# Merge weights spread by one load for two heads, and the output weights loaded in halves: a one-core hybrid decoder step

## The chip, the cores and the metric

The kernel runs on one core of a Trainium2 chip. The metric is the device time of one launch in microseconds (us). The time before is the median of three runs, 3149.05 us (3148.02 to 3153.83). The profile belongs to one further execution, which took 3154.4 us.

## The reference

One layer computes three branches from a normalized input: attention with three dilated patterns per head (A), a convolution (B) and attention to 256 memory tokens (C). Each branch is gated, projected to 1024 columns and merged with a gate; the sum goes through `w_out`, a norm and the residual. Cut to what the change touches:

```python
# branch A: 12 heads of 64; per head three patterns (window, dilation) = (128,1), (512,4), (2048,16)
for (w, d) in PATTERNS:
    o, lse = _dilated_band(qa, ka, va, bias(d), d, w // d)     # o (B,S,H,Dh), lse (B,S,H)
    outs.append(o); lses.append(lse)
wgt = softmax(stack(lses), axis=0)                             # three merge weights per position and head
oa  = einsum('gbshd,gbsh->bshd', stack(outs), wgt)             # branch A's output
...
mix = (gates[..., 0, :] * ((oa * silu(za)) @ w_pa)
     + gates[..., 1, :] * ((ob * silu(zb)) @ w_pb)
     + gates[..., 2, :] * ((oc * silu(zc)) @ w_pc))
y = x + rmsnorm(mix @ w_out, g_post)                           # 2048 prompt rows and 32 sample rows, 1024 wide
```

## The kernel before, in words

Everything is float32. A product is made of three matmuls on a high and a low part of each operand (`gemm`, L166 to L168). The program has three phases. The first (to about 870 us) normalizes the input, makes q, k and v and the convolution's input. The second runs the memory attention, the sample attention and then branch A (about 1600 to 2560 us), while `sweep` fills TensorE's queue with the gate projections (tiles `gg`, weights `whi` and `wlo`, which GpSimd splits at L55 and L56). The third, `phase_c` (2520 us to the end), goes over the positions in four parts of 512 or 544. In each part the branches follow one another in the order C, B, A: the activations `araw` are loaded (L1136) and gated (L1139), split in two (`split_ad`, L1197 on ScalarE and L1198 on VectorE), and eight column blocks are multiplied by the projection weights `craw` (PSUM tile `pg`) and added to `mix` (L1150 to L1155). Then `mix` times `w_out` gives `y` (L1178 to L1180).

Branch A works on six pairs of heads (`att_pair`). A pair's two heads sit in partitions 0 to 63 and 64 to 127 of three tiles `O`, one per pattern. When both heads are done, the softmax statistics go through DRAM and come back as `stc`, and the merge weights `ew` are stored to the DRAM tensor `d_cf`, three rows of 2 x 2048 numbers (L441). They have to be spread: the 64 partitions of a head all need the same row. For each half of the positions (1024) and each pattern (3), a tile `cb` of 128 x 1024 is filled from `d_cf` by two loads, one per head, each of which reads one row of 1024 numbers 64 times (L448). `cb` has two buffers. VectorE multiplies `O` by `cb` for patterns 0 and 1, GpSimd for pattern 2 (L451), and VectorE adds the three (L452, L453) before the result is stored to `d_act` (L454). So a pair takes six `cb` tiles.

A scheduler fixes the order of instructions on each engine before the run; each engine then works through its own list in that order, and an instruction whose data isn't there holds up all behind it. Loads and stores are issued in the same manner: nearly all by SyncE (SP), some by ScalarE (`wraw` and the gates' stores). The next pair's attention starts while the last pair's merge is under way, so its instructions (score matmuls `s` L616 and L617, VectorE's `T` at L625, transposes `pt`, products `o`, splits `pl` at L576, additions to `O` at L644) stand among the merge's on the same engines. The score tiles `s` have two PSUM buffers.

`w_out` (4 MB) is loaded in the first part, after branch A's column blocks in the program text: eight loads of 512 KB into the two buffers of `xr`, each split by ScalarE (L1166) and VectorE (L1167). `xr` also serves the residual input later (L1183).

Of the kernel before, what the change touches and what calls it, by code (L numbers as in the profile page):

```python
# [7 lines left out]
F32 = mybir.dt.float32  # L8
R32 = mybir.dt.float32r
AF = mybir.ActivationFunctionType  # L10
# [5 lines left out]
D = 1024  # L16
S = 2048
# [20 lines left out]
class K:  # L38
# [379 lines left out]
    def att_pair(self, hp):  # L418
        nc, ap, ps, ao = self.nc, self.ap, self.aps, self.ao
        Oraw = [ao.tile([128, S], F32, name="O", bufs=4) for p in range(3)][::-1]  # L420
        bias = self.bias_tiles(hp, ap, ps)
        for a in range(2):
            self.att_head(hp, a, Oraw, {p: t[:, a] for p, t in bias.items()})

        st = ao.tile([32, 6, 128], F32, name="stc")
        for a in range(2):
            nc.sync.dma_start(st[16 * a:16 * a + 16], self.d_st[2 * hp + a].rearrange("g (r i) -> r g i", i=128))
        mn = ao.tile([32, 128], F32, name="mn")
        nc.vector.tensor_tensor(mn, st[:, 0, :], st[:, 1, :], op=ALU.min)
        nc.vector.tensor_tensor(mn, mn, st[:, 2, :], op=ALU.min)  # L430
        e = ao.tile([32, 3, 128], F32, name="ew")
        nc.vector.tensor_tensor(e, st[:, 0:3, :], mn[:, None, :].to_broadcast([32, 3, 128]), op=ALU.subtract)
        nc.scalar.activation(e, e, AF.Exp, scale=-1.0)
        el = st[:, 3:6, :]
        nc.vector.tensor_mul(el, e, el)
        w = ao.tile([32, 128], F32, name="wsum")
        nc.vector.tensor_add(w, el[:, 0, :], el[:, 1, :])
        nc.vector.tensor_add(w, w, el[:, 2, :])
        nc.vector.reciprocal(w, w)
        nc.vector.tensor_tensor(e, e, w[:, None, :].to_broadcast([32, 3, 128]), op=ALU.mult)  # L440
        nc.sync.dma_start(self.d_cf[hp].rearrange("g (q i) -> q g i", i=128), e)  # L441
        for half in range(2):
            cs = slice(half * 1024, half * 1024 + 1024)
            for g in range(3):
                cb = ao.tile([128, 1024], F32, name="cb", bufs=2)
                for a in range(2):
                    src = self.d_cf[hp][g:g + 1, a * S + half * 1024:a * S + half * 1024 + 1024]
                    nc.sync.dma_start(cb[64 * a:64 * a + 64, :],  # L448
                                      bass.AP(tensor=src.tensor, offset=src.offset, ap=[[0, 64], [1, 1024]]))
                eng = nc.gpsimd if g == 2 else nc.vector  # L450
                eng.tensor_mul(Oraw[g][:, cs], Oraw[g][:, cs], cb)  # L451
            nc.vector.tensor_add(Oraw[0][:, cs], Oraw[0][:, cs], Oraw[1][:, cs])  # L452
            nc.vector.tensor_add(Oraw[0][:, cs], Oraw[0][:, cs], Oraw[2][:, cs])  # L453
            nc.sync.dma_start(self.d_act[hp][:, cs], Oraw[0][:, cs])  # L454
# [648 lines left out]
    def phase_c(self):  # L1103
        tc, nc, I, O = self.tc, self.nc, self.I, self.O
        PARTS = [(0, 512, [512]), (512, 512, [512]), (1024, 512, [512]), (1536, 544, [272, 272])]
        with tc.tile_pool(name="cm", side="right", bufs=1, reuse_waits="tile") as mp, \
# [9 lines left out]
            wo = []  # L1116
            xp = I["x_prompt"].rearrange("o (i r) d -> (o r) i d", r=16)
            yp = O["y_p"].rearrange("o (i r) d -> (o r) i d", r=16)
            for s, n, chs in PARTS:
# [11 lines left out]
                for bi, (br, k0, kb, wn) in enumerate(((2, 12, 4, "w_proj_c"), (1, 6, 6, "w_proj_b"), (0, 0, 6, "w_proj_a"))):  # L1131
                    acts = []
                    gn = load_g(br, 0)
                    for k in range(kb):
                        raw = cp.tile([128, 544], F32, name="araw", bufs=2)
# [6 lines left out]
                    for cb in range(8):  # L1142
                        w = self.load_w(wp, I[wn][0, :, 128 * cb:128 * cb + 128], kb, "c", bufs=2, act=True)
                        gs = gn
                        o = 0
# [12 lines left out]
                            gn = load_g(br, cb + 1)  # L1158
                        if bi == 2:
                            mhl.append(self.split_ad(ap, mix[cb], n))  # L1160
                if not wo:
                    for k in range(8):
                        raw = yp_.tile([128, D], F32, name="xr", bufs=2)
                        nc.sync.dma_start(raw, I["w_out"][0, 128 * k:128 * k + 128, :])
                        h, l = ((op if k < 6 else yp_).tile([128, D], R32, name=f"wo{c}{k}") for c in "hl")
                        nc.scalar.activation(h, raw, AF.Copy)  # L1166
                        nc.vector.tensor_sub(l, raw, h.bitcast(F32))  # L1167
                        wo.append((h, l))
                for t0 in range(0, n, 128):
                    m = min(128, n - t0)  # L1170
                    tt = (s + t0) // 128
                    y = psy.tile([128, 2, 512], F32, name="y")
                    ts_ = slice(t0, t0 + m)
                    for c in range(2):
                        cs = slice(512 * c, 512 * c + 512)
                        for k in range(8):
                            (ah, al), (bh, bl) = mhl[k], wo[k]
                            nc.tensor.matmul(y[:m, c, :], ah[:, ts_], bh[:, cs], start=k == 0, stop=False)  # L1178
                            nc.tensor.matmul(y[:m, c, :], ah[:, ts_], bl[:, cs], start=False, stop=False)  # L1179
                            nc.tensor.matmul(y[:m, c, :], al[:, ts_], bh[:, cs], start=False, stop=k == 7)  # L1180
                    yf = y.rearrange("p c d -> p (c d)")
                    xt = yp_.tile([128, D], F32, name="xr", bufs=2)
                    nc.sync.dma_start(xt[:m], xp[tt] if tt < 16 else I["x_sample"].rearrange("b t d -> (b t) d"))  # L1183
                    yt = yp_.tile([128, D], F32, name="yt", bufs=2)
                    ss = yp_.tile([128, 1], F32, name="yss", bufs=2)
                    nc.scalar.activation(yt[:m], yf[:m], AF.Square, accum_out=ss[:m])
                    nc.vector.tensor_scalar(ss[:m], ss[:m], 1.0 / D, 16.0 * EPS, op0=ALU.mult, op1=ALU.add)
                    rs = self.rsqrt(yp_, ss[:m], [128, 1], "yr", None, m)
                    nc.vector.scalar_tensor_tensor(yt[:m], yf[:m], rs, gpost[:m], op0=ALU.mult, op1=ALU.mult)
                    nc.vector.tensor_add(yt[:m], yt[:m], xt[:m])  # L1190
                    nc.sync.dma_start(yp[tt] if tt < 16 else O["y_s"].rearrange("b t d -> (b t) d"), yt[:m])

    def split_ad(self, pool, raw, n):

        nc = self.nc
        h, l = (pool.tile([128, 544], R32, name="ac", bufs=28) for _ in range(2))
        nc.scalar.activation(h[:, :n], raw[:, :n], AF.Copy)  # L1197
        nc.vector.tensor_sub(l[:, :n], raw[:, :n], h[:, :n].bitcast(F32))  # L1198
        return h, l
# [108 lines left out]
```

## Time and profile before

| what | value |
|---|---|
| median of three runs | 3149.05 us |
| profiled execution | 3154.4 us, span of its records 3152.6 us |
| TensorE busy | 3000.2 us, 95% of the span |
| VectorE, ScalarE, GpSimd busy | 64%, 36%, 43% |
| DMA | 454.66 MB, mean 144 GB/s |
| mean granted TensorE clock | 0.979 |

The span is the time from the first to the last record; the execution is 1.8 us longer. Busy times count executing instructions, not waits. In a row of the chain of waits stand the start, the duration and what the chain passed through; in a row by stretches stand the stretch, its length, busy time and count of instructions for each engine, the granted TensorE clock, the busy share of the 16 DMA engines and what they moved. A row of a tile's view gives the line, the engine, the operation, the count, and the least, median and largest duration in ns.

### The profile page before, as it was taken

How to read it: one execution, taken by the hardware profiler on the slowest of the kernel's cores; microseconds unless marked ns; L12 is line 12 of the kernel's file. 1: busy time of each engine (PE TensorE's matmuls, PEld its weight loads, DVE VectorE, ACT ScalarE, POOL GpSimd, SP SyncE). 2: the span in 40 equal slices, each digit the busy share in tenths (PEclk: the TensorE clock that was granted, in tenths of full speed). 3: DMA queues.
4: the chain of work that ended last, by engine and by line, in shares of the span. 5: the costliest groups of instructions: out<-in, count | busy, mean ns of one | idle time of the engine just before them, and what ended most of it. 6: DMA issues, size and time to landing. Idle time of an engine off the chain costs nothing.

```text
span 3152.6 us, 55374 instructions
## 1 busy us (share of the span) xinstructions
PE 3000.2 (95%) x20705; PEld 2839.9 (90%) x20705; DVE 2014.8 (64%) x3734; ACT 1124.2 (36%) x2835; POOL 1350.4 (43%) x1048
## 2 busy tenths in 40 slices
PE   7999999999987999999999999989899979999998
PEld 6899999999987999998999999989898967787897
DVE  5297797796677926465546766666656457556563
ACT  5010010010132433243437575656565523222221
POOL 0121221142356537444256565667676433233240
PEclk9899999999999999999999999999999989999999
DMA  7232222211265454477454656576555487657561
GB/s 250 85 103 80 80 60 61 63 62 50 81 182 167 135 153 144 147 219 239 151 139 116 161 123 163 128 185 150 156 143 152 109 279 227 223 168 227 161 197 53
DMA packets 532218, 454.66 MB, mean 144 GB/s; under 512 B 118191, under 2 KB 458581, under 8 KB 531137
## 3 DMA queue, kind: packets, MB, share of 16 engines
q1 hardware_dynamic: 357502, 335.36, 36.2%
q10 hardware_dynamic: 169840, 105.02, 11.7%
q0 software_dynamic: 4608, 10.75, 1.2%
q8 instruction: 164, 2.69, 0.4%
q14 instruction: 104, 0.85, 0.1%
HBM read 332.96 MB, written 118.04 MB: 143 GB/s over the span
## 4 chain that ended last, share of the span: by engine, by line
PE 70%; DMA 12%; DVE 7%; issue 4%; POOL 3%; ACT 2%; SPq 1%; ACTq 0%; DVEq 0%; POOLq 0%
PE g L166 8%; PE g L167 8%; PE g L168 8%; PE gg L166 6%; PE gg L168 6%; PE gg L167 6%; PE pg L168 3%; PE pg L166 3%; PE pg L167 3%; PE pt L571 2%; DMA cb<-d_cf 2%; PE y L1180 2%; PE y L1179 2%; PE y L1178 2%; PE o L598 1%
## 5 line engine op out<-in xcount | busy, mean ns | idle before, releaser
L166 PE MATMUL gg<-x0h,whi 128*128 128x256 f32 (+1 forms) x2560 | 747.9, 292 | 25.9 <-DVE st L246 12.2
L168 PE MATMUL gg<-x0h,wlo 128*128 128x256 f32 (+1 forms) x2560 | 741.8, 290 | 0.1
L167 PE MATMUL gg<-x0l,whi 128*128 128x256 f32 (+1 forms) x2560 | 741.1, 290 | 0.0
L55 POOL TENSOR_SCALAR whi<-wraw 128x1024 fp32r<-128x1024 f32 x162 | 242.7, 1500 | 928.5 <-PE g L167 524.1
L166 PEld LDWEIGHTS gg<-x0h,whi 128*128 128x128 f32 x2560 | 493.2, 193 | 35.0 <-DVE st L246 13.7
L167 PEld LDWEIGHTS gg<-x0l,whi 128*128 128x128 f32 x2560 | 493.5, 193 | 2.2 <-issue 0.5
L168 PEld LDWEIGHTS gg<-x0h,wlo 128*128 128x128 f32 x2560 | 493.2, 193 | 2.2 <-POOL wlo L56 0.3
L322 DVE SCALAR_TENSOR_TENSOR acc<-G,cw,acc 128x1536 f32<-128x1536 f32 (+15 forms) x354 | 480.8, 1408 | 0.3
L56 POOL TENSOR_TENSOR wlo<-wraw,whi 128x1024 fp32r<-128x1024 f32 x162 | 417.0, 2575 | 9.4 <-PE gg L168 0.2
L155 POOL TENSOR_TENSOR clo<-craw,chi 128x768 fp32r<-128x768 f32 (+1 forms) x96 | 174.1, 1815 | 346.0 <-ACT chi L154 329.8
L627 ACT ACTIVATE P<-T,stm 128x128 f32<-128x128 f32 (+1 forms) x576 | 260.8, 455 | 141.0 <-DVE stm L625 94.8
L239 ACT ACTIVATE st<-g 128x384 f32<-128x384 f32 (+1 forms) x132 | 60.2, 461 | 570.7 <-PE g L168 550.7
L166 PE MATMUL pg<-ac,chi 128*128 128x512 f32 (+1 forms) x640 | 229.4, 359 | 16.6 <-ACT chi L154 8.7
L625 DVE CUSTOM_DVE_ANT_0 T<-s,bias 128x128 f32<-128x128 f32 (+1 forms) x576 | 191.5, 357 | 80.8 <-PE s L617 47.0
L167 PE MATMUL pg<-ac,chi 128*128 128x512 f32 (+1 forms) x640 | 228.8, 358 | 6.3 <-DVE ac L1198 6.3
L168 PE MATMUL pg<-ac,clo 128*128 128x512 f32 (+1 forms) x640 | 227.6, 357 | 3.6 <-POOL clo L155 3.6
L576 DVE TENSOR_TENSOR pl<-pt,ph 128x512 fp32r<-128x512 f32 x240 | 155.6, 652 | 52.4 <-ACT ph L575 48.9
L168 PE MATMUL g<-x0h,wlo 128*128 128x384 f32 x544 | 184.3, 339 | 2.9 <-POOL wlo L56 2.9
L166 PE MATMUL g<-x0h,whi 128*128 128x384 f32 x544 | 183.6, 338 | 2.6 <-ACT st L239 2.3
L167 PE MATMUL g<-x1l,whi 128*128 128x384 f32 x544 | 186.0, 342 | 0.0
L167 PE MATMUL g<-x0l,whi 128*128 128x384 f32 x544 | 185.8, 342 | 0.0
L168 PE MATMUL g<-x1h,wlo 128*128 128x384 f32 x544 | 185.8, 342 | 0.0
(330 smaller groups left out, 7425.0 us busy)
## 6 DMA issues: line engine op xcount, KB each, us to landing
wraw<-in_w_in ACTq DMA_DIRECT2D x119, 512.0 KB
d_g<-st ACTq DMA_DIRECT2D x168, 128.0 KB
cb<-d_cf SPq DMA_DIRECT2D x72, 256.0 KB
g<-d_g SPq DMA_DIRECT2D x72, 256.0 KB
wraw<-in_w_in SPq DMA_DIRECT2D x35, 512.0 KB
kvc<-in_cache_k_win SPq DMA_DIRECT2D x8, 1536.0 KB
kvc<-in_cache_v_win SPq DMA_DIRECT2D x8, 1536.0 KB
raw<-d_q SPq DMA_DIRECT2D x48, 256.0 KB
```

Of the source, the lines that this page charges most:

```text
L55: nc.gpsimd.tensor_scalar(hi, raw, 1.0, 1.0, op0=ALU.mult, op1=ALU.mult)
L56: nc.gpsimd.tensor_sub(lo, raw, hi.bitcast(F32))
L155: nc.gpsimd.tensor_sub(lo, raw, hi.bitcast(F32))
L166: nc.tensor.matmul(ps, hi[:, k, :], h, start=k == 0, stop=False)
L167: nc.tensor.matmul(ps, hi[:, k, :], l, start=False, stop=False)
L168: nc.tensor.matmul(ps, lo[:, k, :], h, start=False, stop=k == kb - 1)
L322: nc.vector.scalar_tensor_tensor(a3[:, lo:hi], G[:, src:src + hi - lo, 2 - m:130 - m], w, a3[:, lo:hi], op0=ALU.mult, op1=ALU.add)
L571: nc.tensor.transpose(t[:, 128 * x:128 * x + 128], pc, self.ident)
L576: nc.vector.tensor_tensor(pl[:, :w], t[:, :w], ph[:, :w].bitcast(F32), op=ALU.subtract)
L625: nc.vector.tensor_tensor_reduce(sc[:, :w], t[:, o:o + w], bias[:, 256 - w:256], 1.0, 3.0e38, ALU.add, ALU.min, m)
L627: nc.scalar.activation(P[:, o:o + w], sc[:, :w], AF.Exp, bias=m, scale=-1.0, accum_out=self.stl[:, col:col + 1])
L1178: nc.tensor.matmul(y[:m, c, :], ah[:, ts_], bh[:, cs], start=k == 0, stop=False)
```

## The change

It has two parts. The two loads of a `cb` tile become one: the source is given as a pattern of three dimensions, two heads (2048 numbers apart), 64 repeats (0 apart) and 1024 numbers, and the destination is the whole tile of 128 partitions. 72 loads of 256 KB become 36 of 512 KB; the bytes are the same. And `w_out` is no longer loaded through `xr`, but in 16 halves of 256 KB through the two buffers of `araw`, one pair of halves with each column block of branch A in the first part.

```diff
--- before.py
+++ after.py
@@ -443,10 +443,8 @@
             cs = slice(half * 1024, half * 1024 + 1024)
             for g in range(3):
                 cb = ao.tile([128, 1024], F32, name="cb", bufs=2)
-                for a in range(2):
-                    src = self.d_cf[hp][g:g + 1, a * S + half * 1024:a * S + half * 1024 + 1024]
-                    nc.sync.dma_start(cb[64 * a:64 * a + 64, :],
-                                      bass.AP(tensor=src.tensor, offset=src.offset, ap=[[0, 64], [1, 1024]]))
+                src = self.d_cf[hp][g:g + 1, half * 1024:half * 1024 + 1024]
+                nc.sync.dma_start(cb, bass.AP(tensor=src.tensor, offset=src.offset, ap=[[S, 2], [0, 64], [1, 1024]]))
                 eng = nc.gpsimd if g == 2 else nc.vector
                 eng.tensor_mul(Oraw[g][:, cs], Oraw[g][:, cs], cb)
             nc.vector.tensor_add(Oraw[0][:, cs], Oraw[0][:, cs], Oraw[1][:, cs])
@@ -1158,14 +1156,8 @@
                             gn = load_g(br, cb + 1)
                         if bi == 2:
                             mhl.append(self.split_ad(ap, mix[cb], n))
-                if not wo:
-                    for k in range(8):
-                        raw = yp_.tile([128, D], F32, name="xr", bufs=2)
-                        nc.sync.dma_start(raw, I["w_out"][0, 128 * k:128 * k + 128, :])
-                        h, l = ((op if k < 6 else yp_).tile([128, D], R32, name=f"wo{c}{k}") for c in "hl")
-                        nc.scalar.activation(h, raw, AF.Copy)
-                        nc.vector.tensor_sub(l, raw, h.bitcast(F32))
-                        wo.append((h, l))
+                            if s == 0:
+                                wo.append(self.load_wo(cb, cp, op if cb < 6 else yp_))
                 for t0 in range(0, n, 128):
                     m = min(128, n - t0)
                     tt = (s + t0) // 128
@@ -1190,6 +1182,17 @@
                     nc.vector.tensor_add(yt[:m], yt[:m], xt[:m])
                     nc.sync.dma_start(yp[tt] if tt < 16 else O["y_s"].rearrange("b t d -> (b t) d"), yt[:m])
 
+    def load_wo(self, k, cp, pool):
+
+        nc = self.nc
+        h, l = (pool.tile([128, D], R32, name=f"wo{c}{k}") for c in "hl")
+        for o in (0, 512):
+            raw = cp.tile([128, 544], F32, name="araw", bufs=2)[:, :512]
+            nc.sync.dma_start(raw, self.I["w_out"][0, 128 * k:128 * k + 128, o:o + 512])
+            nc.scalar.activation(h[:, o:o + 512], raw, AF.Copy)
+            nc.vector.tensor_sub(l[:, o:o + 512], raw, h[:, o:o + 512].bitcast(F32))
+        return h, l
+
     def split_ad(self, pool, raw, n):
 
         nc = self.nc
```

The scheduler makes a new order of this. SyncE's list at the first pair's merge (`d_cf` the merge weights, `cb` their spread tiles, `rv` the next head's values, `d_act` the merged result), before:

```order
L441 DMA d_cf_108<-ew 32x3x128
L448 DMA cb<-d_cf_108 64x1024 x8
L545 DMA rv<-out_v_win_p 8x16x64 x4
L448 DMA cb<-d_cf_108 64x1024 x4
L454 DMA d_act_114<-O 128x1024
L545 DMA rv<-out_v_win_p 8x16x64 x12
L454 DMA d_act_114<-O 128x1024
```

and with the change (the load of `cb` is L447 now, and the lines behind it have numbers two less):

```order
L441 DMA d_cf_108<-ew 32x3x128
L447 DMA cb<-d_cf_108 128x1x1024 x4
L543 DMA rv<-out_v_win_p 8x16x64 x4
L447 DMA cb<-d_cf_108 128x1x1024 x2
L543 DMA rv<-out_v_win_p 8x16x64 x2
L452 DMA d_act_114<-O 128x1024
L543 DMA rv<-out_v_win_p 8x16x64 x10
```

Twelve loads are now six, at the same place among their neighbours.

VectorE's list at the same merge, with the change (L449 is the multiplication by `cb`, L450 and L451 the additions, the others are the next pair's attention):

```order
L449 TENSOR_TENSOR O<-O,cb 128x1024
L623 ISA T,stm<-s,bias_13448 128x256
L623 ISA stm 128x1
L449 TENSOR_TENSOR O<-O,cb 128x1024
L642 TENSOR_TENSOR O<-o,ot 64x512
L574 TENSOR_TENSOR pl<-pt,ph 128x512
L450 TENSOR_TENSOR O<-O 128x1024
```

These seven rows read the same before, with L451, L625, L644, L576 and L452 for the lines: the multiplications keep their places between the next pair's instructions.

SyncE's list at the first loads of `w_out` (the projection weights are `craw`, gates `g`), before:

```order
L1115 DMA gpost<-in_g_post 128x1024
L1136 DMA araw<-d_actb 128x512
L1164 DMA xr<-in_w_out 128x1024 x2
L1138 DMA z<-d_zb_84 128x512
L1127 DMA g<-d_g_143 128x512
L150 DMA craw<-in_w_proj_c 128x4x128
```

and with the change:

```order
L1136 DMA z<-d_zc_89 128x512
L1191 DMA araw<-in_w_out 128x512 x2
L1125 DMA g<-d_g_138 128x512
L150 DMA craw<-in_w_proj_b 128x6x128
L150 DMA craw<-in_w_proj_a 128x6x128
L1191 DMA araw<-in_w_out 128x512 x2
```

The loads of `w_out` moved from beside the weights of branch C (`w_proj_c`) to beside those of branch A (`w_proj_a`).

## The prediction

> **What bounds the kernel now.** I read the page first, then the six stretches in which a pair's merge runs, then the chain of waits inside them, and last whatever the trace tells of how a load is shared among the DMA engines. The page:
>
> ```profile
> span 3152.6 us, 55374 instructions
> PE 3000.2 (95%) x20705; PEld 2839.9 (90%) x20705; DVE 2014.8 (64%) x3734; ACT 1124.2 (36%) x2835; POOL 1350.4 (43%) x1048
> PE 70%; DMA 12%; DVE 7%; issue 4%; POOL 3%; ACT 2%; SPq 1%; ACTq 0%; DVEq 0%; POOLq 0%
> ```
>
> TensorE bounds the kernel: it is busy for 95% of the span, so 152 us of idle time is all that any change of waits can win. To lose time there is no such limit. The six merges, from a pair's first `cb` load to its last addition (stretch, length, busy time and count by engine, granted clock, DMA share, GB/s):
>
> ```profile
> core 0: us, PE busy (x) PEld busy (x) DVE busy (x) ACT busy (x) POOL busy (x), PEclk, DMA share, GB/s
> 1775.80:1803.00 27.20, 23.99 (x195) 23.79 (x194) 22.39 (x54) 17.71 (x56) 11.69 (x6) 0.94 0.75 185
> 1920.00:1950.00 30.00, 26.95 (x223) 26.37 (x223) 22.14 (x60) 16.66 (x56) 15.22 (x9) 0.98 0.80 184
> 2066.00:2094.00 28.00, 26.91 (x212) 26.71 (x211) 22.45 (x59) 17.75 (x60) 14.30 (x13) 0.91 0.78 187
> 2223.00:2250.00 27.00, 21.99 (x169) 21.40 (x169) 21.46 (x46) 12.97 (x42) 13.12 (x8) 0.94 0.72 190
> 2376.00:2404.00 28.00, 23.70 (x170) 23.05 (x169) 20.32 (x47) 13.78 (x46) 11.72 (x8) 0.88 0.75 167
> 2535.00:2563.00 28.00, 19.92 (x132) 18.31 (x130) 11.26 (x10) 4.05 (x9) 11.88 (x6) 0.82 0.73 201
> sum 168.20, PE 143.46 PEld 139.62 DVE 120.01 ACT 82.92 POOL 77.93; mean PE 23.91 PEld 23.27 DVE 20.00 ACT 13.82 POOL 12.99
> ```
>
> A merge takes 28 us on average and TensorE loses 4 of them (168.20 - 143.46 = 24.7 us in all six). Each merge is a chain of loads and multiplications; the first and the last pair's:
>
> ```profile
> 1774.13 1.70 DMA d_cf<-ew
> 1776.34 4.29 DMA cb<-d_cf
> 1780.73 2.41 DVE O L451
> 1794.90 4.92 DMA cb<-d_cf
> ...
> 2536.40 4.85 DMA cb<-d_cf
> 2543.54 4.87 DMA cb<-d_cf
> 2557.26 1.23 DVE O L452
> ```
>
> and the tile's own view (line, engine, operation, least, median, largest ns; then a wait that ended with it, us and times):
>
> ```profile
> L448 SPq DMA_DIRECT2D cb<-d_cf x72: 444/588/1565, 1775.8 to 2553.6; - x72
> L451 DVE TENSOR_TENSOR O<-O,cb x24: 1202/1226/3441, 1780.7 to 2556.0; 128x1024 f32<-128x1024 f32 x24
> L451 POOL TENSOR_TENSOR O<-O,cb x12: 2349/2524/3438, 1789.1 to 2559.3; 128x1024 f32<-128x1024 f32 x12
>   DMA cb<-d_cf: 112.1, 24
> ```
>
> A pair of 256-KB loads lands within 4.3 to 4.9 us, and already engines stand 112.1 us in all waiting for `cb`, nearly all of it covered by other engines' work.
>
> **How a load is shared.** The DMA engines are sixteen, and the first part of the change alters how many of them a load can use. One place in the trace tells of that, near the end of the input stage (sizes in KB first, then the chain there, then a small load of the first merge):
>
> ```profile
> cw_rows<-in_conv_w SPq DMA_DIRECT2D x1, 93.0 KB
> rbr<-in_rel_bias SPq DMA_DIRECT2D x1, 1.5 KB
> ...
> 86.49 0.25 SPq L91
> 86.80 6.72 DMA rbr<-in_rel_bias
> ...
> 1763.87 1.87 DMA stc<-d_st
> ```
>
> `rbr`, 1.5 KB, took 6.72 us, where `stc`, 48 KB, takes 1.87. It was issued right behind `cw_rows` (L91), 93 KB in 31 rows. Spread over all engines 93 KB would be gone in a fraction of a microsecond; I read the row as `cw_rows` lying on one engine, with the piece of `rbr` that goes to this engine queued behind. 31 rows cannot be dealt out evenly to 2, 4, 8 or 16 engines; every load of the attention has 8, 16, 32, 64 or 128 rows outermost. The new `cb` load has an outermost source count of 2 (two heads), with the 64 repeats inside. By this reading it can be dealt out to two engines only, one per head, where each old load (64 repeats outermost) went to sixteen.
>
> The Trainium skill states this as a rule ("DMA: Bandwidth & Descriptors", section "Why a DMA increments its semaphore by 16 and not by 1"): each side's slowest dimension other than 1 is looked at, and the largest number up to 16 that divides both is the number of engines. It gives 16 for the old loads (64 and 64), 2 for the new one (2 and 128) and 1 for `cw_rows` (31); with the last the 6.72 us agree, and no run here shows the second yet. The same page's section "Bandwidth" advises batching into larger DMAs, which speaks for the change; no row here bears that out for 512 KB.
>
> **The price of one new load.** Two engines carry 256 KiB each, 262,144 bytes. What does one engine move? The best stretch for loads with long rows, while the input is read:
>
> ```profile
> 2.00:6.00 4.00, 0.00 (x0) 0.00 (x0) 0.00 (x0) 1.28 (x4) 0.00 (x0) 1.00 0.93 340
> ```
>
> 340 / (16 x 0.93) = 22.8 GB/s for a busy engine: 11.5 us a load. From `cw_rows`: 93 KB are 95,232 bytes in 6.72 - 1.87 = 4.85 us, 19.6 GB/s: 13.3 us. From the six merges, where many rows are short: mean 186 GB/s at a mean share of 0.755, 15.4 GB/s: 17.0 us. The new load keeps rows of 4 KB and is nearest to the first, but the two engines also carry their sixteenth of the other traffic; I take 12.5 and keep 11.5 and 17.0 for the range. (By the skill's fabric figure in "Bandwidth", 435.2 GB/s over 16, it would be 9.6 us, an estimate, and the total 3341.)
>
> **The merges.** All six loads of a pair now queue on the same two engines. Two buffers let two be under way, so the engines never rest, and the six follow one another. A merge then takes 0.45 us of issue, 1.87 of a load's fixed time (the `stc` row), six transfers, 2.52 for GpSimd's last multiplication and 1.23 for the last addition: 6c + 6.1 us. With c = 12.5 that is 81 us against 28. Over six pairs: 6 x 81.1 - 168.2 = **+318 us**.
>
> Does TensorE lose all of this? Behind the waiting multiplication on VectorE stands the next pair's attention: in the list shown with the change, one score step between the first two multiplications, a few more before the next. TensorE's list interleaves the score matmuls with the gate projections, and with two score buffers it stops at the third step that VectorE hasn't taken. The nearest row for the slack (TensorE waiting for VectorE's score step: us in total, times, longest):
>
> ```profile
> PE s L616 <- DVE stm L625: 10.3, 6, 3.2
> ```
>
> I allow one such longest stall per merge, 3.2 us, as work done ahead: -19 us. Between merges TensorE has no idle time in which to make up the rest. In the last merge the multiplications stand with no attention left between them, and branch C's `ac` splits (L1198) wait behind them, so there TensorE stops too. SyncE is held as well, at the third `cb` load until the first multiplication frees a buffer; behind it stand `rv` and the next `raw` loads, whose consumers are late by the same time. That costs nothing of its own.
>
> The 36 issues saved on SyncE, 0.588 us each, are worth nothing once the two engines set the pace.
>
> **The output weights.** The stretches of branch C and B's start, and of branch A, in the first part; then the splits of `w_out` before, and those of the same shape as the new ones:
>
> ```profile
> 2569.00:2618.00 49.00, 39.71 (x152) 29.79 (x150) 39.04 (x45) 21.11 (x27) 17.89 (x11) 0.93 1.03 349
> 2618.00:2664.00 46.00, 45.08 (x195) 36.55 (x196) 33.17 (x35) 14.88 (x21) 22.64 (x13) 1.00 0.67 206
> ...
> L1166 ACT ACTIVATE woh<-xr x8: 1041/1049/1062, 2574.4 to 2605.1; 128x1024 fp32r<-128x1024 f32 x8
> L1167 DVE TENSOR_TENSOR wol<-xr,woh x8: 1211/1218/2857, 2575.5 to 2607.4; 128x1024 fp32r<-128x1024 f32 x8
> ...
> L1197 ACT ACTIVATE ac<-araw x64: 613/632/662, 2551.1 to 3017.1; 128x512 fp32r<-128x512 f32 x48, 128x544 fp32r<-128x544 f32 x16
> L1198 DVE TENSOR_TENSOR ac<-araw,ac x64: 679/693/1786, 2558.4 to 3017.8; 128x512 fp32r<-128x512 f32 x48, 128x544 fp32r<-128x544 f32 x16
> ```
>
> Now the DMA engines are full from 2569 to 2618 and TensorE idles for 9.3 us; 4 MB of that go 50 us later, where the engines are at 0.67 and 4 MB more in 46 us (91 GB/s) bring them near 0.94. ScalarE's 8 x 1.05 = 8.4 us become 16 x 0.63 = 10.1, VectorE's 8 x 1.22 = 9.8 become 16 x 0.69 = 11.0; VectorE has 46 - 33.2 = 12.8 us free there, just enough. Gain between 9 (all the early idle time) and a loss of 9 (the same stall handed to branch A); I take **-4 us**.
>
> **Sum.** 3154.4 (the profiled execution) + 318 - 19 - 4 = 3449; that execution was 5.4 us above the median, so **3444 us**. With c = 11.5 the merges add 282 and the sum is 3408; with c = 17.0 they add 480 and it is 3606.
>
> **Rivals.**
> *The load still goes over all sixteen engines.* Then it is one 512-KB load for two of 256 KB: two to three `cb` waits per pair lie on the chain and each loses an issue of 0.588 us, 6 x 2.5 x 0.588 = 9 us, and with the 4 us the time is about 3136, faster. It decides if the dealing follows the destination's 128 rows. The page's 112.1 us of waiting speak for a gain by it, `cw_rows` against it. Chance 0.08 (0.05 faster by over 0.2%; the remaining 0.03 that the new order eats the gain). Larger batches, as the skill advises, would be this case.
> *TensorE covers half.* Before, VectorE and GpSimd waited 112.1 us and TensorE lost 24.7. Were the gate projections ahead of the blocked score steps deep enough to hide half of the 318 us, the time is 3149 + 159 - 4 = 3304. Against it: its list is fixed and there are two score buffers. Chance 0.12.
> *The two engines hold back everything.* Every other load has a piece on them, behind up to two `cb` loads: `rv`, `raw` and the gate weights come late, TensorE's own filler stops, and c goes to 17 or beyond: 3606 and more. Chance 0.12.
> *The forecast*, between 3408 and 3606: 0.68.
>
> What a measurement can tell from no change is about 0.2%, 6 us. Slower: 0.68 + 0.12 + 0.12 = 0.92; the same 0.03; faster 0.05. The range takes in the forecast's own, 3408 to 3606, and most of the second rival: 3330 to 3610.
>
> **What would show it.** Each merge lasting 70 to 110 us in the stretches, with the DMA share falling to about 0.2 to 0.4 and GB/s to under 100; `cb` pieces of 11 us and more on the chain, and with 8% or more of the span; TensorE losing 40 to 60 us per merge; everything before 1774 us unchanged. In the output weights: less idle time just after branch C's start and no wait of `y` for `woh` or `wol`. I am wrong in kind if a `cb` load still lands in about 5 us, and wrong in size if it takes 12 us but the merges overlap with TensorE's work.

## Result and profile after

The changed kernel took 3428.79 us, the median of six runs (3427.0 to 3436.28), against 3148.53 us of the kernel before (six runs, 3136.91 to 3162.22). The ratio is 1.089, with a 95% interval of 1.0866 to 1.0915. The prediction was 3444 us, in a range from 3330 to 3610. The loss has the sign and nearly the size that was expected; the parts of the sum are another matter, as the account below shows.

The page of the kernel after: span, busy time of the engines, shares of the chain that ended last by engine and by line:

```profile
span 3427.9 us, 55321 instructions
PE 3039.7 (89%) x20705; PEld 2877.4 (84%) x20705; DVE 2004.6 (58%) x3742; ACT 1126.8 (33%) x2843; POOL 1343.6 (39%) x1048
PE 64%; DMA 19%; DVE 7%; issue 4%; POOL 3%; SPq 2%; ACT 2%; ACTq 0%; DVEq 0%; POOLq 0%
DMA cb<-d_cf 8%; PE g L166 7%; PE g L167 7%; PE g L168 7%; PE gg L166 6%; PE gg L168 6%; PE gg L167 6%; DMA rv<-out_v_win_p 2%; PE pg L168 2%; PE pt L569 2%; PE pg L166 2%; PE pg L167 2%; PE y L1171 2%; PE y L1172 2%; PE y L1170 2%
```

TensorE executes as many matmuls as before (20705), and its share falls from 95% to 89%. Its idle time is 3427.9 - 3039.7 = 388.2 us, where it was 152.4. DMA has 19% of the chain, where it had 12%, and the new first line of it is the load of `cb`, with 8% of the span.

The six merges of the kernel after, each from the first issue of a `cb` load to the last addition, by stretches (columns as in the prediction's table):

```profile
1770.60:1845.50 74.90, 33.11 (x204) 32.07 (x203) 21.75 (x56) 17.47 (x56) 11.88 (x8) 0.71 0.21 70
1959.90:2038.40 78.50, 36.01 (x226) 34.98 (x224) 20.52 (x47) 14.76 (x47) 14.26 (x9) 0.71 0.23 74
2155.40:2235.10 79.70, 32.45 (x195) 30.88 (x194) 22.84 (x62) 18.90 (x61) 15.29 (x17) 0.66 0.29 85
2353.90:2433.30 79.40, 33.98 (x197) 33.13 (x197) 23.81 (x61) 17.66 (x58) 15.96 (x10) 0.68 0.22 72
2551.60:2626.40 74.80, 31.05 (x191) 30.02 (x191) 21.44 (x49) 14.69 (x49) 14.40 (x9) 0.67 0.23 77
2745.00:2824.20 79.20, 34.66 (x233) 33.37 (x231) 9.68 (x9) 5.75 (x13) 19.00 (x11) 0.71 0.29 96
sum 466.50, PE 201.25 PEld 194.46 DVE 120.04 ACT 89.23 POOL 90.79; mean PE 33.54 PEld 32.41 DVE 20.01 ACT 14.87 POOL 15.13
```

And the kernel before, cut at the same two events of each merge:

```profile
1775.80:1805.20 29.40, 25.74 (x208) 25.33 (x206) 24.40 (x56) 18.31 (x57) 13.89 (x8) 0.94 0.72 179
1922.10:1951.50 29.40, 26.07 (x217) 25.28 (x217) 21.91 (x52) 16.60 (x55) 16.24 (x10) 1.00 0.85 197
2069.60:2108.10 38.50, 32.58 (x247) 31.20 (x246) 27.21 (x60) 20.47 (x61) 22.73 (x25) 0.90 0.98 220
2223.40:2254.40 31.00, 25.99 (x202) 25.40 (x201) 24.07 (x52) 15.07 (x47) 16.24 (x8) 0.94 0.73 189
2378.10:2408.20 30.10, 25.80 (x185) 25.10 (x183) 21.04 (x45) 14.77 (x46) 12.67 (x7) 0.89 0.81 190
2535.90:2563.20 27.30, 19.22 (x125) 17.60 (x124) 11.46 (x11) 3.67 (x9) 10.98 (x6) 0.81 0.73 199
sum 185.70, PE 155.40 PEld 149.91 DVE 130.07 ACT 88.89 POOL 92.75; mean PE 25.90 PEld 24.98 DVE 21.68 ACT 14.82 POOL 15.46
```

A merge now takes 77.8 us instead of 30.9, and while it lasts the DMA engines are busy for 21 to 29% and move 70 to 96 GB/s. TensorE is idle for 466.50 - 201.25 = 265.3 us in these stretches, 44 us a merge, against 30.3 before. The granted clock falls to 0.66 to 0.71. The sum of before is 185.7 us and not the 168.20 of the prediction: the stretches quoted there ended at round times, and the third at 2094, when its last addition was at 2108.1.

The chain of waits in the first merge of the kernel after:

```profile
1771.23 22.06 DMA cb<-d_cf
...
1794.57 21.75 DMA cb<-d_cf
...
1817.60 13.04 DMA cb<-d_cf
```

and its first two multiplications in VectorE's timeline (start, us, line, shapes; in brackets the idle time before it and what ended it):

```profile
1782.84 1.22 DVE L449 TENSOR_TENSOR O<-O,cb 128x1024 f32<-128x1024 f32 x1 [9.90 <-DMA cb<-d_cf]
1793.32 1.23 DVE L449 TENSOR_TENSOR O<-O,cb 128x1024 f32<-128x1024 f32 x1 [8.91 <-DMA cb<-d_cf]
```

The 22.06 us hold two loads, one behind the other. The first multiplication starts at 1782.84 us, 11.6 us after the start of the wait, and the second at 1793.32, 10.48 us later; before, a pair of loads landed in 4.29. Two engines carry 262,144 bytes each per load: in 10.48 us that is 25.0 GB/s per engine. While one tile is multiplied (1.23 us) the next load is already under way, until the fifth: that one is issued only at 1817.60 us, when the fourth has landed and been used.

That it is two engines can be read from the DMA share. A stretch of this merge in which only `cb` loads were moving:

```profile
1776.00:1784.00 8.00, 0.00 (x0) 0.00 (x0) 1.16 (x2) 0.00 (x0) 2.88 (x2) 0.63 0.13 52
```

Two of sixteen engines are 0.125 of them; the row shows 0.13, at 52 GB/s, and not one matmul in 8 us.

The tile's own view, with the engines that wait for it:

```profile
  DMA cb<-d_cf: 611.0, 36
  POOL O L449: 330.1, 12
  DVE O L449: 280.9, 24
```

Every one of the 36 multiplications now waits for its load, 611.0 us in all on two engines, where before 24 of them waited 112.1 us.

How that reaches TensorE, by its waits over the whole span (us in all, times, longest):

```profile
PE s L614 <- DVE stm L623: 93.6, 9, 15.3
...
PE pg L167 <- DVE ac L1201: 15.8, 1, 15.8
```

The wait of a score matmul for VectorE's score step has grown from 10.3 to 93.6 us. These are the next pair's instructions behind the waiting multiplications in VectorE's list. In the last merge it is branch C's split `ac` (L1201) that stands there, and TensorE's first products of that branch wait 15.8 us for it.

The whole difference of the two profiled executions, by parts (cut at the unrounded events, so that a last digit can differ from the sums above):

| part of the span, us | before | after | difference |
|---|---|---|---|
| to the first `cb` issue | 1775.8 | 1770.6 | -5.2 |
| the six merges | 185.6 | 466.5 | +280.9 |
| between the merges | 601.7 | 587.1 | -14.6 |
| after the last merge | 589.5 | 603.6 | +14.1 |
| span | 3152.6 | 3427.9 | +275.3 |

### The profile page after: what moved, and what is told of

The parts are those of the page before. It is cut to its first block, busy times and chain, and to the rows that moved or that the text cites. A ratio compares the mean times of both kernels' runs of the same rounds, so it can differ in the third digit from the quotient of the medians.

```text
span 3427.9 us, 55321 instructions
## 1 busy us (share of the span) xinstructions
PE 3039.7 (89%) x20705; PEld 2877.4 (84%) x20705; DVE 2004.6 (58%) x3742; ACT 1126.8 (33%) x2843; POOL 1343.6 (39%) x1048
## 4 chain that ended last, share of the span: by engine, by line
PE 64%; DMA 19%; DVE 7%; issue 4%; POOL 3%; SPq 2%; ACT 2%; ACTq 0%; DVEq 0%; POOLq 0%
DMA cb<-d_cf 8%; PE g L166 7%; PE g L167 7%; PE g L168 7%; PE gg L166 6%; PE gg L168 6%; PE gg L167 6%; DMA rv<-out_v_win_p 2%; PE pg L168 2%; PE pt L569 2%; PE pg L166 2%; PE pg L167 2%; PE y L1171 2%; PE y L1172 2%; PE y L1170 2%
## 5 line engine op out<-in xcount | busy, mean ns | idle before, releaser
L166 PE MATMUL gg<-x0h,whi 128*128 128x256 f32 (+1 forms) x2560 | 755.7, 295 | 38.0 <-ACT st L243 20.1
L167 PE MATMUL gg<-x0l,whi 128*128 128x256 f32 (+1 forms) x2560 | 751.2, 293 | 0.0
L166 PEld LDWEIGHTS gg<-x0h,whi 128*128 128x128 f32 x2560 | 502.1, 196 | 46.1 <-ACT st L243 19.6
L168 PEld LDWEIGHTS gg<-x0h,wlo 128*128 128x128 f32 x2560 | 502.0, 196 | 12.3 <-POOL wlo L56 10.4
L167 PEld LDWEIGHTS gg<-x0l,whi 128*128 128x128 f32 x2560 | 502.5, 196 | 2.0 <-issue 0.5
L625 ACT ACTIVATE P<-T,stm 128x128 f32<-128x128 f32 (+1 forms) x576 | 260.6, 454 | 305.6 <-DVE stm L623 217.3
L614 PE MATMUL s<-KH,QS 128*128 128x128 f32 (+1 forms) x576 | 168.6, 314 | 104.6 <-DVE stm L623 93.6
L167 PE MATMUL pg<-ac,chi 128*128 128x512 f32 (+1 forms) x640 | 229.0, 358 | 15.8 <-DVE ac L1201 15.8
L595 PE MATMUL o<-ph,V 128*128 128x128 f32 (+1 forms) x612 | 165.2, 284 | 74.0 <-DVE O L642 41.4
L614 PEld LDWEIGHTS s<-KH,QS 128*128 128x128 f32 x576 | 117.2, 204 | 106.9 <-DVE stm L623 95.7
L449 DVE TENSOR_TENSOR O<-O,cb 128x1024 f32<-128x1024 f32 x24 | 29.4, 1225 | 280.9 <-DMA cb<-d_cf 280.9
L595 PEld LDWEIGHTS o<-ph,V 128*128 128x128 f32 x612 | 122.9, 203 | 76.5 <-issue 42.2
```

The lines of the kernel that those rows point to most:

```text
L166: nc.tensor.matmul(ps, hi[:, k, :], h, start=k == 0, stop=False)
L167: nc.tensor.matmul(ps, hi[:, k, :], l, start=False, stop=False)
L168: nc.tensor.matmul(ps, lo[:, k, :], h, start=False, stop=k == kb - 1)
L595: nc.tensor.matmul(o, vb, ph[:, 128 * x:128 * (x + cnt)], start=first, stop=False, skip_group_check=True)
L614: nc.tensor.matmul(t[:, o:o + w], q, keys(KH, jj), start=True, stop=False)
L625: nc.scalar.activation(P[:, o:o + w], sc[:, :w], AF.Exp, bias=m, scale=-1.0, accum_out=self.stl[:, col:col + 1])
```

## The experiments

Three questions were open: which part of the change costs the time; whether the outermost count of the source sets how many DMA engines a load uses; and what the output weights' new place is worth. The kernels of an experiment leave nothing of the computation out.

**Each part alone.** `load_only` has the one load for two heads and `w_out` as before; `wout_only` has the two loads and the new way of `w_out`.

> The change without its second part: one load per cb tile, w_out whole through xr as before. Theory: the merges last 75 to 80 us each and the time is that of the full change plus the 4 us that moving w_out may be worth, 3425 to 3440 us. Rival (w_out's move is a share of the loss): under 3415 us.

> The change without its first part: two loads per cb tile as before, w_out in halves through araw. Theory (the single load on two DMA engines is all of the loss): about 3144 us, between 3139 and 3157; the merges last 27 to 39 us as before, and TensorE's idle time behind branch C's start falls from about 9 us to about 5. Rival (moving w_out costs something of its own, hidden in the 280 us): 3160 us or more, with idle time of TensorE in branch A of the first part.

`load_only` took 3434.88 us, 1.0901 times the kernel before (1.0885 to 1.0917): the whole loss. Its merges add up to 466.3 us, and the multiplications wait 610.6 us for the tile, 36 times, as in the kernel after.

`wout_only` took 3154.92 us, 1.0011 times (1.0002 to 1.0019): no gain of 4 us, rather a loss below what can be told from no change. Its merges are those of before, 185.2 us.

**The same bytes, the repeats written in two dimensions.** These three kernels keep the kernel before (two loads per `cb`, one per head, 64 repeats of one row) and alter only how the 64 repeats are written in the source's pattern. The bytes, the rows of 4 KB and the number of loads stay as they are. From the top, the lines of `two_2x32`, `two_4x16` and `two_8x8`:

```diff
-                                      bass.AP(tensor=src.tensor, offset=src.offset, ap=[[0, 64], [1, 1024]]))
+                                      bass.AP(tensor=src.tensor, offset=src.offset, ap=[[0, 2], [0, 32], [1, 1024]]))
+                                      bass.AP(tensor=src.tensor, offset=src.offset, ap=[[0, 4], [0, 16], [1, 1024]]))
+                                      bass.AP(tensor=src.tensor, offset=src.offset, ap=[[0, 8], [0, 8], [1, 1024]]))
```

> The kernel before, with two loads of 256 KB per cb tile, but each writes its 64 repeats as 2 x 32 (both with step 0). Bytes, rows, destinations and the number of loads stay. Theory (the outermost count of the source sets the number of engines): two engines again, both heads' loads behind one another on them, merges of 75 to 82 us and 3400 to 3450 us. Rival (the slowness belongs to the one large load, or to stepping between the heads): as before, 3149 us, merges near 30 us.

> As the run with 2 x 32, but 4 x 16. Theory: four engines, a tile's transfer takes half of 12 us, merges of 6 x 6 + 6 = 42 us (38 to 48) against 31 before, 3149 + 6 x 11 = 3215 us (3185 to 3255). Rival (any source with a dimension outside the 64 repeats is slow, whatever its count): as with 2 x 32, about 3430 us. Rival (the large load alone is slow): 3149 us.

> The kernel before, with the 64 repeats of each of the two loads written as 8 x 8. Theory (outermost count sets the engines): eight engines. The runs with 2 and 4 gave merges of 78 and 49 us, transfers of 12.0 and 7.2 us a tile; on a line in 1/engines eight give 4.8 us, merges of 35 us against 31 before, and 3151 + 6 x 4 = 3175 us (3155 to 3195). Rival (a dimension outside the repeats costs by itself): 3250 us or more.

| outermost count | time, us | ratio to before | mean merge, us | wait for `cb`, us |
|---|---|---|---|---|
| 64 (before) | 3149.71 and 3150.94, the medians beside these runs | 1 | 30.9 | 112.1 |
| 8 | 3188.95 | 1.0134 (1.0106 to 1.0162) | 37.8 | 176.0 |
| 4 | 3257.9 | 1.034 (1.0318 to 1.0362) | 49.1 | 264.9 |
| 2 | 3442.05 | 1.0924 (1.0901 to 1.0947) | 78.8 | 613.3 |

The first merge by stretches, in `two_2x32`:

```profile
1776.40:1856.50 80.10, 32.42 (x208) 31.34 (x206) 21.80 (x56) 18.30 (x57) 12.01 (x8) 0.73 0.20 66
```

in `two_4x16`:

```profile
1774.90:1822.80 47.90, 28.52 (x209) 27.44 (x207) 21.82 (x56) 18.43 (x57) 11.96 (x8) 0.84 0.36 109
```

and in `two_8x8`:

```profile
1770.80:1806.30 35.50, 27.77 (x209) 26.69 (x207) 22.50 (x56) 18.34 (x58) 13.06 (x8) 0.90 0.59 146
```

The same work of about 209 matmuls lies in all three, and in the 29.40 us of before. The DMA share goes 0.20, 0.36, 0.59 (0.72 before) and the granted clock 0.73, 0.84, 0.90 (0.94). These shares hold other loads too. Stretches of the same merges in which only `cb` loads were moving tell the number of engines; from the top `two_2x32`, `two_4x16` and `two_8x8`:

```profile
1784.00:1792.00 8.00, 0.00 (x0) 0.00 (x0) 1.20 (x2) 0.00 (x0) 0.66 (x1) 0.66 0.13 51
1780.00:1784.00 4.00, 0.34 (x3) 0.13 (x2) 0.00 (x0) 0.00 (x0) 3.28 (x2) 0.91 0.26 92
1776.00:1780.00 4.00, 0.79 (x7) 0.58 (x6) 2.15 (x3) 0.52 (x2) 4.00 (x2) 1.00 0.52 124
```

Of sixteen engines 0.13 is two, 0.26 is four and 0.52 is eight. So the number of engines is set by the source's outermost count (the destination has 64 or 128 rows throughout), and the two-head load isn't slow because it is one load or 512 KB: written with an outermost 2, two loads of 256 KB are as slow. This is the rule of the Trainium skill ("DMA: Bandwidth & Descriptors", section "Why a DMA increments its semaphore by 16 and not by 1") that the prediction set beside the `cw_rows` row, and the runs agree with it for 2, 4 and 8.

The price falls less than by half with each doubling. By the prediction's form for a merge, 6c + 6.1 us, a tile costs c = 12.1, 7.2 and 5.3 us at 2, 4 and 8 engines and 4.1 before. The 3257.9 us of `two_4x16` lie just above what was expected of it. One reason is in the three rows: a busy engine moves 51 / (16 x 0.13) = 24.5 GB/s where two engines are at work, 92 / (16 x 0.26) = 22.1 where four are, and 124 / (16 x 0.52) = 14.9 where eight are. More engines on the same rows are each slower; why, no run here shows. The form also counts all six transfers in a row, so that with faster loads the multiplications are a larger part of c.

Both loads of a tile go to the *same* engines: `two_2x32` has one load for each head, so with engines of their own the two would have used four, and its merges would be near the 49.1 us of `two_4x16`. They take 78.8 us, as in the change (77.8), where the one load has both heads, and the share is 0.13 and not 0.25.

**One load over sixteen engines.** If the outermost count is the cause, a single load for both heads with an outermost 16 must land as fast as the old pair. `one_16src` stores the merge weights eight times per head and lets the load read 16 rows, each repeated 8 times:

```diff
-        nc.sync.dma_start(self.d_cf[hp].rearrange("g (q i) -> q g i", i=128), e)
+        for a in range(2):
+            for g in range(3):
+                nc.sync.dma_start(self.d_cf[hp][g, a * 8 * S:(a + 1) * 8 * S].rearrange("(k r i) -> r k i", k=8, i=128),
+                                  e[16 * a:16 * a + 16, g, :][:, None, :].to_broadcast([16, 8, 128]))
...
+                nc.sync.dma_start(cb, bass.AP(tensor=src.tensor, offset=src.offset, ap=[[S, 16], [0, 8], [1, 1024]]))
```

> One load of 512 KB per cb tile, as in the change, w_out as before; but each head's merge weights are stored eight times in DRAM, so that the load's source is 16 rows with step, 8 repeats of each, 1024 numbers: outermost count 16. The store of the weights becomes six of 64 KB instead of one of 48 KB. Theory: the single load goes over sixteen engines, merges near 31 us plus 2 to 4 us for the six stores, 3155 to 3180 us. Rival (one load for both heads is slow because it is one large load, or one with both heads' rows): merges of 75 us, 3400 us and more.

It took 3164.3 us, 1.0056 times the kernel before (1.0036 to 1.0076). The first merge by stretches:

```profile
1782.00:1809.60 27.60, 24.68 (x200) 24.50 (x199) 21.23 (x48) 15.07 (x47) 13.28 (x8) 0.94 0.81 194
```

and the chain of waits at its start:

```profile
1779.09 0.42 SPq L443
...
1779.56 2.44 DMA d_cf<-ew
...
1782.02 5.02 DMA cb<-d_cf
```

One load of 512 KB lands in 5.02 us, and while it moves the engines are full:

```profile
1784.00:1787.00 3.00, 3.00 (x28) 2.99 (x26) 0.00 (x0) 2.20 (x5) 2.97 (x3) 1.00 1.00 236
```

The six merges take 181.5 us, 4 less than before. So one load for two heads is no loss in itself. Nor is it a gain: there are 36 issues of loads fewer but 30 of stores more, and the 4 us won in the merges are lost outside them. Ahead of the merge the chain has issues of the stores (L443) and the last one's 2.44 us, where before it had one store of 1.70; the parts outside the merges are together 3162.1 - 181.5 = 2980.6 us, against 2967.0. How much of these 13.6 us is the stores' was not measured by itself. A pattern that spreads both heads over sixteen engines without the extra copies was not run.

**The output weights.** The branches C, B and A of the first part, cut at the same matmuls. Before:

```profile
2551.80:2593.80 42.00, 28.61 (x97) 21.22 (x98) 25.42 (x32) 13.48 (x19) 11.54 (x7) 0.80 0.90 298
2593.80:2631.20 37.40, 34.28 (x146) 26.60 (x145) 31.91 (x34) 14.20 (x19) 16.52 (x8) 1.00 0.96 314
2631.20:2664.50 33.30, 33.30 (x145) 27.00 (x144) 23.70 (x25) 11.34 (x17) 15.58 (x9) 1.00 0.60 178
```

`wout_only`:

```profile
2549.60:2586.60 37.00, 27.16 (x97) 20.65 (x98) 20.93 (x27) 8.16 (x13) 11.48 (x7) 0.82 0.87 281
2586.60:2621.40 34.80, 34.09 (x146) 26.73 (x145) 27.38 (x31) 12.59 (x18) 16.05 (x8) 1.00 0.89 276
2621.40:2660.60 39.20, 35.35 (x146) 26.43 (x145) 28.55 (x37) 17.15 (x27) 17.32 (x9) 1.00 0.76 230
```

In these executions, one of each kernel, branches C and B win 5.0 and 2.6 us, 7.6 together, with the loads of `w_out` gone from beside theirs (DMA share 0.90 and 0.96 before, 0.87 and 0.89 now). Branch A gives 5.9 back: 39.20 us where it took 33.30 without a gap in TensorE's work. A round of the ring in its chain of waits:

```profile
2627.18 3.43 DMA araw<-in_w_out
...
2630.64 0.64 ACT woh L1194
...
2631.30 0.85 DVE wol L1195
...
2632.18 2.82 DMA araw<-in_w_out
```

and TensorE's waits in branch A and in the first blocks of `y`:

```profile
PE pg L168 <- POOL clo L155: 3.8, 7, 0.9
PE y L1172 <- DVE yt L1183: 2.4, 1, 2.4
```

A half is loaded, split on ScalarE, split on VectorE, and its buffer is then free for the next load: about 5 us a round (2627.18 to 2632.18). From 2619.99 to 2657 the chain holds nothing but these rounds. TensorE loses 3.8 us to the projection weights `clo`, seven times a little, and its busy time there is 2.05 us longer for one matmul more; together that is the 5.9. The projection weights stand between the halves in SyncE's list, and each half's load waits for a buffer of the ring; that this is what makes `clo` late is my reading and wasn't tried alone. That would leave 1.7 us won, and a wait of 2.4 us follows that wasn't there before: at 2687 us the third block of `y` waits until VectorE has read the first (L1183). VectorE does that at 2685.64 us, as before (2685.74), although `y` began at 2660.45 and not at 2664.33. So what is won up to `y` is lost in it.

`wout_own_A` asks whether the shared ring is the fault, and gives the halves two buffers of their own:

```diff
-            raw = cp.tile([128, 544], F32, name="araw", bufs=2)[:, :512]
+            raw = cp.tile([128, 512], F32, name="wh", bufs=2)
```

> As the run with only the move of w_out, two loads per cb tile, but the halves have two buffers of their own of 128 x 512 instead of araw's. The scheduler then starts them at branch C and spreads them over all three branches of the first part. Theory (in branch A the halves wait for one another through araw's two buffers, each round of load, copy and subtraction 4.9 us, and hold up SyncE's list with the projection weights): branch A takes 33 us again instead of 39, the early idle time lies between the two, and the time is 3144 to 3153 us. Rival (any place beside the branches costs the same DMA time): 3151 us within 0.2%, with the stall in another branch.

It took 3152.17 us, 1.0016 times (1.0003 to 1.0028): no gain either. The issues of the halves' loads:

```profile
L1193 SPq DMA_DIRECT2D wh<-in_w_out x16: 332/333/582, 2516.7 to 2600.6; - x16
```

and the three branches by stretches:

```profile
2546.60:2588.60 42.00, 28.31 (x97) 20.61 (x98) 29.06 (x38) 13.29 (x22) 10.99 (x7) 0.80 0.92 303
2588.60:2628.20 39.60, 36.62 (x146) 28.89 (x145) 30.89 (x38) 14.22 (x21) 16.70 (x9) 0.91 0.89 284
2628.20:2661.50 33.30, 33.30 (x145) 26.98 (x145) 24.02 (x24) 11.30 (x17) 16.39 (x9) 1.00 0.57 175
```

With buffers of its own the scheduler issued the loads from 2516.7 on, and the last at 2600.6, before branch A had begun. So branch A is whole again (33.30 us) and branch C as long as before (42.00). The experiment moved the loads back as it freed the ring, and so it doesn't say what the ring costs alone. The rival of the expectation came true: the stall moved to another branch. Beside the late place, the early one costs C and B 9.8 us more (81.6 and 71.8 us together) and branch A 5.9 less.

## Why the prediction was right, and where its numbers were off

**The load goes to two engines.** Right, and shown: the reading of one row (`rbr` behind `cw_rows`) held for the outermost counts 2, 4 and 8, and the DMA shares show the engines themselves. The row itself was read rightly, too. In the single transfers of the trace before, the 31 rows of `cw_rows` move one after another from 87.39 to 92.83 us; 30 of the 32 rows of `rbr` (48 bytes each) are through by 88 us, and the last two start at 92.84, right behind them. The first rival, a load that still goes over sixteen, fell with the result, and the three patterns and `one_16src` show why.

**The merges, +318.** Right in mechanism, 37 us too large, in two halves. With 11.94 us a transfer, from (466.5 / 6 - 6.1) / 6, and not 12.5, the six merges are 466.5 and not 486.6 us: 20 us. And the merges before were cut 17.4 us short, since I cut the stretches at round times and did not look up the last addition in each. 318 - 20 - 17 = 281, which is the measured +280.9. The choice of 12.5 was an allowance of one microsecond over the best row (11.5) for other traffic. Over a whole merge a load took 11.94 us, 22.0 GB/s per engine, and 22.8 was in that row; a load with little beside it took 10.48 us, 25.0 GB/s, so the 9.6 us that stood beside the sum as an estimate were not reached. In the first merge the two engines also rested before the fifth load, where the prediction had them never rest. The far row (17.0) was of no use, and its reason, short rows, is not needed: in `one_16src` sixteen engines at work on 4-KB rows alone moved 236 / 16 = 14.8 GB/s each.

**Work ahead, -19.** This step failed. The matmuls inside the merges went from 1184 to 1246 in the rows' counts (208 + 217 + 247 + 202 + 185 + 125, and 204 + 226 + 195 + 197 + 191 + 233), and in the first five merges they fell, from 1059 to 1013. In `two_2x32`, which keeps the order of before, the six counts are 208, 195, 232, 214, 193 and 137, together 1179. So in merges that are two and a half times as long TensorE did no more of the next pair's work; that it stops at the same instruction of its list however long the stop is fits these counts and is inferred from them. In the new order only the last merge has more, by 108. The time between merges is 14.6 us less, and the time after the last merge 14.1 us more, so that nothing is left of it. Both belong to the new order and not to the wait: `two_2x32`, with the order of before and merges of 473.0 us, has 600.3 us between them and 591.1 after them, while `load_only`, with the new order, has 585.2 and 603.1. In the order of before two of branch C's `ac` splits stand ahead of the last addition, in the new one all of them behind it. So branch C's row of matmuls begins 12 us before the last merge ends in `two_2x32` (2837.5 and 2849.7 us), and in the kernel after it begins when the merge has ended (2824.9 and 2824.2).

**What TensorE loses.** I had asked for 40 to 60 us a merge; it is 44. Busy time rose as well, by 39.5 us for the same 20705 matmuls. By the rows, a matmul in the merges took 155.40 / 1184 = 0.1313 us before and 201.25 / 1246 = 0.1615 after, at a granted clock that fell from a mean of 0.91 to 0.69: 1246 x 0.0302 = 38 us. So the rival by which TensorE covers half falls: the merges hold 201 us of it, but some 38 of the 46 that were added are the same work, slower.

**The two engines hold back everything, 3606 and more.** They do hold SyncE back (the last section), and `rv` has a larger part of the chain, but c stayed at 11.9, and the stretches between the merges did not grow. That rival fell.

**The output weights, -4.** Not gained. It was taken between +9 and -9, from idle time at C's start and from the same stall handed to A, and the second of these is what took the gain: 7.6 us won, 5.9 given back in branch A and the rest at the third block of `y`. VectorE's spare time, which I had called just enough, is not where the chain goes in branch A: it goes round the ring. Neither `woh` nor `wol` is waited for by `y`, as expected. In the whole change the part is below what can be told: the intervals of the kernel after (1.0866 to 1.0915) and of `load_only` (1.0885 to 1.0917) overlap.

**The rest.** The 36 issues saved are worth nothing beside the two engines, as said; `one_16src` doesn't price them, since its stores cost more. Up to the first `cb` issue nothing changed that can be told: it comes at 1770.6 us, and in the six other kernels that are the same up to there it comes between 1770.8 and 1778.2.

With the measured terms the sum is 3152.6 - 5.2 + 280.9 - 14.6 + 14.1 = 3427.8, the span of the kernel after. The prediction had +295 for the span's +275.3: 37 too much in the merges, 18.5 and 4 too much gain in the other two terms, and 5.2 by which this execution began its merges earlier. Errors of both signs met, so the closeness of the total says little for the single terms.

## What to carry to other kernels

When a load is given more dimensions, look at the outermost one: here a source with an outermost 2 used two DMA engines, and the same bytes took 78.8 us a merge instead of 30.9. Two loads that begin with 64 rows each are better than one that begins with two heads; to join them, put a count of 16 outermost, as `one_16src` does. A large count isn't enough by itself: the 31 rows of `cw_rows` lay on one engine. And when a term is the difference of two stretches, cut both at the same events, and ask whether the work "done ahead" is new work or the same list stopped at the same place.

## What the hardware showed that was not expected

In the kernel after, loads that are issued behind the `cb` loads don't only land late: their *issue* takes long, and SyncE stands still. The loads of `rv` on SyncE (least, median, largest ns) in the kernel after:

```profile
L543 SPq DMA_DIRECT2D rv<-out_v_win_p x192: 272/323/9785, 1644.7 to 2690.8; - x192
```

and before:

```profile
L545 SPq DMA_DIRECT2D rv<-out_v_win_p x192: 272/322/1134, 1650.4 to 2468.3; - x192
```

and a row of SyncE's timeline in the first merge of the kernel after (start, us, engine, line):

```profile
1795.16 14.22 SPq L543 DMA_DIRECT2D rv<-out_v_win_p  x4
```

Four issues that take 0.3 us each in the median took 14.22 us together; why an issue takes that long, the runs don't show. The prediction had SyncE held only by the wait for a free buffer, at no cost. The chain now gives `rv` 2% of the span (83 us, where it had 24.5 before), but the stretches between the merges are not longer, so no cost of its own is shown; where a queue carries the loads of the next stage, such a stop could be one.

The second was the granted clock. It was lower where the wait was longer: 0.94, 0.90, 0.84, 0.73 and 0.71 in the first merges of the kernel before, of `two_8x8`, of `two_4x16`, of `two_2x32` and of the kernel after (the last two wait about equally long). In the four that keep the order, the same 208 or 209 matmuls took 25.74, 27.77, 28.52 and 32.42 us. So matmuls in a merge with long waits were slower, too, which hides nothing of the wait but makes the busy time look like work. What sets the clock wasn't tried by itself.
